# A hybrid decoder trunk: gates and branch products with tokens on partitions, 512 features at a time

## The chip, the cores and the metric

The kernel runs on one core of one Trainium2 chip. The metric is the device time of one launch in microseconds (us). A core has TensorE (PE in the profile; its weight loads have a row of their own, PEld), VectorE (DVE), ScalarE (ACT), GpSimd (POOL) and SyncE (SP, which here issues the loads). SBUF has 128 partitions; TensorE writes to PSUM alone, and its results are read from there by VectorE or ScalarE.

## What is computed

Two layers; in each, three attention mixers, merged by gates, then an output projection, and an MLP. All is float32, with 256 tokens and 1024 features. The part that the change touches, cut from the reference:

```python
h = _rms_norm(x, norm_mix_pre[l])
proj = jnp.einsum('bsd,de->bse', h, w_in[l])
dq, dk, dv, mq, mk, mv, c_q, c_kv, k_pe, g = jnp.split(proj, IN_OFFSETS, axis=-1)
... # oa, ob, oc: the three mixers, each (B, S, 512)
branches = jnp.stack([oa, ob, oc], axis=2)
br = jnp.einsum('bsgc,gcd->bsgd', branches, w_branch[l])   # w_branch: (3, 512, 1024)
gates = jax.nn.sigmoid(g.reshape(B, S, N_BRANCH, D_MODEL)) # 3 x 1024 features
mixed = jnp.einsum('bsd,de->bse', jnp.sum(gates * br, axis=2), w_out[l])
x = x + _rms_norm(mixed, norm_mix_post[l])
```

## The kernel before

**Products in three parts.** Each float32 weight is split into two float32r parts: the high part by a ScalarE copy (L129), the low part by a VectorE subtraction (L130), both 1024 columns wide, once for each load (`chunk`, L132). A product is then three matmuls into one PSUM tile: high by high (L176), high by low (L177), low by high (L178), by `mm3` and `mm_group`. The loads go through 5 raw buffers, and the parts through 6 buffers for high and 6 for low.

**Two layouts of a product.** In `load_f` (L167) a load is 4 blocks of 128 rows by 256 columns, the weights are the operand that stays (128 columns), and the activations move, 256 tokens at a time: the result has features on partitions. In `load_t` (L159) a load is 2 blocks of 128 rows by 512 columns, the activations stay (128 tokens), and 512 columns of weights move: the result has tokens on partitions. Either way a matmul is 128 by 128 stationary, and a layout needs no transposed copy of the activations, which lie with features on partitions.

**The stage.** In `mixer`, L624 to 660, for each of four blocks of 256 features and three branches: a gate product over 8 blocks of rows (PSUM tile `pg`, 48 matmuls of 256 columns), multiplied on VectorE by the tokens' 1/rms, which lies along the free axis (`rb2`, L639), into a gate tile of 512 columns `g`. Then, again for each feature block and branch: the sigmoid of the gate on ScalarE (L646), the branch product over 4 blocks of rows (`pb`, 24 matmuls), its product with the gate on VectorE into `br` (L653), and sums over branches on GpSimd (L657). The sum, which already has features on partitions, is split into the high and low part of `mixed` (ScalarE L659, VectorE L660). The output projection (`out_proj`, tiles `po`, 512 columns, tokens on partitions) takes `mixed` as its stationary operand, two of its eight row blocks in each of four `mixed` tiles.

**What sets the order.** A scheduler at build time places the instructions on each engine by a timeline of its own, and after that each engine keeps its order. It puts gate products between the steps of the attention, as filler for TensorE; the stage after the attention is gate products, then branch products, then the output projection. Three of the last five `w_out` loads put their parts in buffers of the gate pool (6 buffers of 1024 columns, L701).

Of the kernel before, what the change touches and what calls it, by code (L numbers as in the profile page):

```python
# [9 lines left out]
F32 = mybir.dt.float32  # L10
# [3 lines left out]
AF = mybir.ActivationFunctionType  # L14
OP = mybir.AluOpType

D = 1024
# [12 lines left out]
            2.7524476990947733e-06, -2.3874981991411914e-08)  # L30
# First relative distance of each T5 bucket that distances 0..255 can reach.
BUCKET_START = tuple(range(17)) + (21, 27, 35, 46, 59, 77, 99, 128, 166, 216)
# [3 lines left out]
def trunk(ctx: ExitStack, tc: tile.TileContext, x, positions, rel_bias, norm_mix_pre, norm_mix_post,  # L36
# [45 lines left out]

# [1 line left out]
    # Rows of vectors that act on features once those lie on partitions.  # L84
    n_rows = 16 + 16 + 4 + 2 + 2
# [37 lines left out]

# [1 line left out]
    def split(dst_hi, dst_lo, src, quick=False):  # L125
# [6 lines left out]
    def chunk(src, nk, c, name, parts=None, spare=None, quick=False):  # L132
        """One load of weights and its two parts; `spare` is a pool that is idle now."""
        n = nk * c
# [24 lines left out]
    def load_t(w2d, c0, c, name, kts=KT):  # L159
        """Weights that move: kts tiles of [128, c]."""  # L160
        nk = 1024 // c
        r = []
        for k0 in range(0, kts, nk):
            r += chunk(wslice(w2d, k0, nk, c0, c), nk, c, f"{name}_{k0}")
        return r

    def load_f(w2d, c0, name, kts=KT):  # L167
        """Weights that stay: two blocks of 128 columns, kts tiles each."""
        r = []
        for k0 in range(0, kts, 4):  # L170
            r += chunk(wslice(w2d, k0, 4, c0, 256), 4, 256, f"{name}_{k0}")
        return [[(h[:, b * 128:(b + 1) * 128], l[:, b * 128:(b + 1) * 128]) for h, l in r] for b in range(2)]
# [15 lines left out]

# [1 line left out]
    def new_act(name):  # L190
# [40 lines left out]
    def post_norm(xt, ps2, wpost, eps_col):  # L231
        """x += rms_norm(ps2) * wpost"""
        parts = small_tile("pnp", 2)
# [18 lines left out]

# [1 line left out]
    bias = consts.tile([128, 9, 256], F32, name="bias")  # L254
# [22 lines left out]
    def setup_rope():  # L277
# [11 lines left out]
        for t in range(2):  # L289
            for j in range(2):  # L290
                V.tensor_scalar(ang[:, t, j, :], fr, pf[:, t:t + 1], None, op0=OP.mult)
        # Index 0: sine.  Index 1: cosine, the sine a quarter turn on.
        V.tensor_scalar(k[:, :, 0, :], ang[:, :, 0, :], 1.0 / math.pi, MAGIC, op0=OP.mult, op1=OP.add)
# [23 lines left out]
    def setup_lam():  # L317
# [10 lines left out]
        for l in range(DEPTH):  # L328
            li = 0.8 - 0.6 * math.exp(-0.3 * l)
            nc.vector.tensor_scalar(lam[:, l:l + 1], dots[:, 2 * l:2 * l + 1], dots[:, 2 * l + 1:2 * l + 2], li,  # L330
                                    op0=OP.subtract, op1=OP.add)
            # The weights come out of the chip negated: the sign goes here.
            nc.vector.tensor_scalar(subc[:, l:l + 1], cols[:, 38 + l:39 + l], -(1.0 - li), None, op0=OP.mult)

# [1 line left out]
    last_exp = [None]  # L336
# [35 lines left out]
    def av_f(ps, pt, v0, v1):  # L372
        """ps [c, 256 queries] = v^T p^T"""
        nc.tensor.matmul(ps, v0, pt[:, 0:256], start=True, stop=False)
        nc.tensor.matmul(ps[:, 128:256], v1, pt[:, 256:384], start=False, stop=True)

# [1 line left out]
    def load_c(l, k1, n):  # L378
# [5 lines left out]
    def mixer(l, xs, tiles, wc, before):  # L384
# [6 lines left out]

        # latent queries, keys and the shared rope key, token-major
        wc = wc or load_c(l, 0, 4)
# [30 lines left out]

        # 1/rms of every token along the free axis, on all partitions
        prb = tr_tile("prb")
# [24 lines left out]

        # transposed latents
        def latents():
# [20 lines left out]

        # differential attention
        o_a = []
# [44 lines left out]

        # block attention: one block holds the whole sequence, so each query sees its own block
        mv = v_proj(OFF['mv'], "mv")
# [14 lines left out]

        # latent attention
        uq = []  # L540
# [85 lines left out]

        # gates and the products of the three branches, two feature blocks at a time
        branches = [[(o[j // 2][:, 0, j % 2, :], o[j // 2][:, 1, j % 2, :]) for j in range(4)] for o in (o_a, o_b, o_c)]
        gs = {}
        for d in range(4):  # L630
            if d % 2 == 0:
                gt2 = [gpool.tile([128, 2, 512], F32, tag="g", name="g") for _ in range(3)]
            for b in range(3):
                w = load_f(win, OFF['g'] + b * D + d * 256, f"g{l}{b}{d}")
                pg = mm_tile("pg")
                for j in range(2):
                    mm_group(pg[:, j * 256:(j + 1) * 256], w[j], act)
                gt = gt2[b][:, d % 2, :]
                nc.vector.tensor_tensor(gt.rearrange("p (b s) -> p b s", b=2), pg.rearrange("p (b s) -> p b s", b=2),  # L639
                                        rb2, op=OP.mult)  # L640
                gs[b, d] = gt
        mixed = new_act("mixed")
        for d in range(4):
            m = None
            for b in range(3):
                i = nc.scalar.activation(gs[b, d], gs[b, d], AF.Sigmoid)  # L646
                order_after(i, sig_after)
                w = load_f(w_branch[l, b], d * 256, f"br{l}{b}{d}", kts=4)
                pb = acc_tile("pb")
                for j in range(2):  # L650
                    mm_group(pb[:, j * 256:(j + 1) * 256], w[j], branches[b])
                r = prep_tile("br")
                nc.vector.tensor_tensor(r, pb[:], gs[b, d], op=OP.mult)  # L653
                if m is None:
                    m = r
                else:
                    nc.gpsimd.tensor_tensor(m, m, r, op=OP.add)  # L657
            mv_ = m.rearrange("p (b s) -> p b s", b=2)
            nc.scalar.activation(mixed[d][:, 0], mv_, AF.Copy)  # L659
            nc.vector.tensor_tensor(mixed[d][:, 1], mv_, mixed[d][:, 0].bitcast(F32), op=OP.subtract)  # L660

        # output projection
        wpost = load_post(norm_mix_post, l, sig_after)
# [14 lines left out]
    def finish(accs, held, xs, wpost, eps_cols, nxt, wcol, stored=None):  # L678
        """The last rows of a projection, the first half of the tokens ahead, and the norm that follows."""
        for t in range(2):  # L680
# [14 lines left out]
    def out_proj(l, w2d, act, wpost, xs):  # L695
        """x += rms_norm(mixed @ w_out); the next block's input follows each half of the tokens."""
        tiles = new_act("h2")
# [143 lines left out]
```

## Time and profile before

| what | value |
|---|---|
| median of 3 runs | 875.62 us (873.63 to 876.04) |
| the profiled execution: span from its first to its last instruction | 874.3 us |
| TensorE: busy, matmuls | 858.1 us (98%), 5820 |
| weight loads of TensorE | 791.0 us (90%) |
| VectorE, ScalarE, GpSimd busy | 62%, 54%, 12% |
| DMA: read, mean rate | 151.19 MB, 175 GB/s |
| granted clock of TensorE, mean of the span | 0.997 of full |

The profile gives no time of the profiled execution beside its span. A matmul's duration on the page is from its issue to a modelled end, and matmuls overlap: for what one costs in a full queue, the time from one start to the next is read, in the view of instructions in order of time.

### The profile page before, as it was taken

What the parts mean: (1) busy time and instruction counts of PE and PEld (TensorE: products, weight loads), DVE (VectorE), ACT (ScalarE), POOL (GpSimd) and SP (SyncE); (2) the same over time, 40 slices, a digit from 0 to 9 for tenths busy, and PEclk for the clock granted to TensorE, in tenths of its full rate; (3) what the DMA queues carried; (4) which work ended last, traced back from release to release, by engine and by line L of the source; (5) the groups of instructions that cost most, each with busy time, mean ns of one, the idle gap of its engine ahead of it and who ended that gap; (6) DMA issues with size and microseconds to landing.
All of it is one profiled execution on the core that took longest, in us unless ns stands there. A gap on an engine that the chain in (4) does not pass through costs nothing.

```text
span 874.3 us, 14960 instructions
## 1 busy us (share of the span) xinstructions
PE 858.1 (98%) x5820; PEld 791.0 (90%) x5820; DVE 539.6 (62%) x921; ACT 468.9 (54%) x820; POOL 107.1 (12%) x130
## 2 busy tenths in 40 slices
PE   7999999999999999999999999999999999999997
PEld 6988999899988999999899899999998899999995
DVE  6757688457867445446575768954578754554452
ACT  6536675644546444445464757664544664444441
POOL 2211210001311000000100012000033010000010
PEclk9999999999999999999999999999999999999999
DMA  8865544356666656667738553546558466665631
GB/s 275 260 168 180 144 124 134 107 178 184 203 232 195 185 182 189 191 193 212 228 97 248 146 149 97 150 117 189 177 187 270 145 218 191 192 193 182 186 115 49
DMA packets 109798, 154.27 MB, mean 176 GB/s; under 512 B 5103, under 2 KB 89136, under 8 KB 109728
## 3 DMA queue, kind: packets, MB, share of 16 engines
q1 hardware_dynamic: 108448, 149.70, 56.4%
q10 hardware_dynamic: 608, 2.11, 0.7%
q0 software_dynamic: 672, 1.51, 0.6%
q8 instruction: 46, 0.75, 0.4%
q14 instruction: 24, 0.20, 0.1%
HBM read 151.19 MB, written 2.11 MB: 175 GB/s over the span
## 4 chain that ended last, share of the span: by engine, by line
PE 88%; issue 4%; DMA 3%; DVE 2%; ACT 1%; POOL 1%; SPq 0%; POOLq 0%; DVEq 0%; ACTq 0%
PE pu L176 7%; PE pu L178 7%; PE pu L177 7%; PE pd L177 6%; PE pd L178 6%; PE pd L176 6%; PE pg L176 5%; PE pg L177 5%; PE pg L178 5%; PE pb L178 3%; PE pb L177 3%; PE pb L176 3%; PE pmqk L178 2%; PE pmqk L177 2%; PE pmqk L176 2%
## 5 line engine op out<-in xcount | busy, mean ns | idle before, releaser
L177 PE MATMUL pu<-h,hi_up 128*128 128x256 f32 x448 | 126.9, 283 | 0.0
L178 PE MATMUL pu<-h,lo_up 128*128 128x256 f32 x448 | 126.8, 283 | 0.0
L176 PE MATMUL pu<-h,hi_up 128*128 128x256 f32 x448 | 126.7, 283 | 0.0
L130 DVE TENSOR_TENSOR lo_wd<-raw_wd,hi_wd 128x1024 fp32r<-128x1024 f32 x64 | 77.7, 1225 | 74.5 <-ACT hi_wd L129 74.5
L129 ACT ACTIVATE hi_wd<-raw_wd 128x1024 fp32r<-128x1024 f32 x64 | 67.0, 1058 | 82.6 <-PE pu L177 38.0
L176 PE MATMUL pg<-h,hi_g 128*128 128x256 f32 x384 | 110.6, 288 | 0.4 <-ACT lqk L602 0.4
L178 PE MATMUL pg<-h,lo_g 128*128 128x256 f32 x384 | 109.7, 286 | 0.0
L177 PE MATMUL pg<-h,hi_g 128*128 128x256 f32 x384 | 109.1, 284 | 0.0
L130 DVE TENSOR_TENSOR lo_up<-raw_up,hi_up 128x1024 fp32r<-128x1024 f32 x64 | 80.2, 1258 | 38.8 <-ACT hi_up L129 38.5
L129 ACT ACTIVATE hi_up<-raw_up 128x1024 fp32r<-128x1024 f32 x64 | 67.9, 1064 | 59.5 <-PE pu L177 29.0
L176 PE MATMUL pd<-hi_wd,u 128*128 128x512 f32 x256 | 99.9, 390 | 0.0
L177 PE MATMUL pd<-lo_wd,u 128*128 128x512 f32 x256 | 99.8, 390 | 0.0
L178 PE MATMUL pd<-hi_wd,u 128*128 128x512 f32 x256 | 99.6, 389 | 0.0
L176 PEld LDWEIGHTS pu<-h,hi_up 128*128 128x128 f32 x448 | 85.9, 192 | 0.6
L177 PEld LDWEIGHTS pu<-h,hi_up 128*128 128x128 f32 x448 | 85.9, 192 | 0.5
L178 PEld LDWEIGHTS pu<-h,lo_up 128*128 128x128 f32 x448 | 85.9, 192 | 0.1
L130 DVE TENSOR_TENSOR lo_g<-raw_g,hi_g 128x1024 fp32r<-128x1024 f32 x48 | 58.6, 1222 | 39.0 <-ACT hi_g L129 38.7
L176 PEld LDWEIGHTS pg<-h,hi_g 128*128 128x128 f32 x384 | 73.5, 191 | 1.4 <-ACT lqk L602 0.6
L177 PEld LDWEIGHTS pg<-h,hi_g 128*128 128x128 f32 x384 | 73.5, 191 | 0.5 <-issue 0.3
L178 PEld LDWEIGHTS pg<-h,lo_g 128*128 128x128 f32 x384 | 73.5, 191 | 0.1
L129 ACT ACTIVATE hi_g<-raw_g 128x1024 fp32r<-128x1024 f32 x48 | 50.5, 1057 | 40.2 <-PE pg L177 32.2
L752 POOL TENSOR_TENSOR r<-r 128x512 f32<-128x512 f32 x28 | 30.6, 1094 | 262.1 <-ACT u L751 230.9
(293 smaller groups left out, 2109.2 us busy)
## 6 DMA issues: line engine op xcount, KB each, us to landing
raw_up<-in_w_up_dram SPq DMA_DIRECT2D x64, 512.0 KB, 3.9
raw_wd<-in_w_down_dram SPq DMA_DIRECT2D x64, 512.0 KB, 4.2
raw_g<-in_w_in_dram SPq DMA_DIRECT2D x48, 512.0 KB, 3.8
raw_br<-in_w_branch_dram SPq DMA_DIRECT2D x24, 512.0 KB, 4.1
raw_dqk<-in_w_in_dram SPq DMA_DIRECT2D x16, 512.0 KB, 5.2
raw_mqk<-in_w_in_dram SPq DMA_DIRECT2D x16, 512.0 KB, 4.1
raw_wo<-in_w_out_dram SPq DMA_DIRECT2D x16, 512.0 KB, 3.9
raw_dv<-in_w_in_dram SPq DMA_DIRECT2D x8, 512.0 KB, 4.9
```

Source lines behind the costliest of these rows:

```text
L129: nc.scalar.activation(dst_hi, src, AF.Copy)
L130: nc.vector.tensor_tensor(dst_lo, src, dst_hi.bitcast(F32), op=OP.subtract)
L176: i = nc.tensor.matmul(ps, sh, mh, start=first, stop=False)
L177: nc.tensor.matmul(ps, sh, ml, start=False, stop=False)
L178: nc.tensor.matmul(ps, sl, mh, start=False, stop=last)
L752: nc.gpsimd.tensor_tensor(r, r, r, op=OP.mult)
```

## The change

The gates and the branch products go from `load_f` to `load_t`: tokens on partitions, 512 features in one matmul. A gate tile is now two token tiles of 512 features for each half of the features and each branch; its 1/rms is one number for each partition, so a ScalarE copy with a scale (L637) takes over from the VectorE multiplication. The product with the gate is written in place into the gate tile, GpSimd sums in place, and the sum, which has tokens on partitions, is transposed on TensorE (four 128 by 128 transposes for each half and token tile, PSUM tile `pmx`, L657) and split into `mixed` from there (L662, L663). The comments of the file are left out too. The core of the diff:

```diff
-        for d in range(4):
-            if d % 2 == 0:
-                gt2 = [gpool.tile([128, 2, 512], F32, tag="g", name="g") for _ in range(3)]
+        for hf in range(2):
             for b in range(3):
-                w = load_f(win, OFF['g'] + b * D + d * 256, f"g{l}{b}{d}")
-                pg = mm_tile("pg")
-                for j in range(2):
-                    mm_group(pg[:, j * 256:(j + 1) * 256], w[j], act)
-                gt = gt2[b][:, d % 2, :]
-                nc.vector.tensor_tensor(gt.rearrange("p (b s) -> p b s", b=2), pg.rearrange("p (b s) -> p b s", b=2),
-                                        rb2, op=OP.mult)
-                gs[b, d] = gt
+                w = load_t(win, OFF['g'] + b * D + hf * 512, 512, f"g{l}{b}{hf}")
+                gt2 = gpool.tile([128, 2, 512], F32, tag="g", name="g")
+                for t in range(2):
+                    pg = mm_tile("pg")
+                    mm_group(pg[:], toks(act, t), w)
+                    nc.scalar.activation(gt2[:, t, :], pg[:], AF.Copy, scale=rr[:, t:t + 1])
+                    gs[hf, b, t] = gt2[:, t, :]
...
-                w = load_f(w_branch[l, b], d * 256, f"br{l}{b}{d}", kts=4)
-                pb = acc_tile("pb")
-                for j in range(2):
-                    mm_group(pb[:, j * 256:(j + 1) * 256], w[j], branches[b])
-                r = prep_tile("br")
-                nc.vector.tensor_tensor(r, pb[:], gs[b, d], op=OP.mult)
...
-            mv_ = m.rearrange("p (b s) -> p b s", b=2)
-            nc.scalar.activation(mixed[d][:, 0], mv_, AF.Copy)
-            nc.vector.tensor_tensor(mixed[d][:, 1], mv_, mixed[d][:, 0].bitcast(F32), op=OP.subtract)
+                w = load_t(w_branch[l, b], hf * 512, 512, f"br{l}{b}{hf}", kts=4)
+                for t in range(2):
+                    g = gs[hf, b, t]
+                    i = nc.scalar.activation(g, g, AF.Sigmoid)
+                    order_after(i, sig_after)
+                    pb = acc_tile("pb")
+                    mm_group(pb[:], toks(branches[b], t), w)
+                    nc.vector.tensor_tensor(g, pb[:], g, op=OP.mult)
+                    if b:
+                        m = gs[hf, 0, t]
+                        nc.gpsimd.tensor_tensor(m, m, g, op=OP.add)
+            for t in range(2):
+                m = gs[hf, 0, t]
+                pt = tr_tile("pmx")
+                for j in range(4):
+                    nc.tensor.transpose(pt[:, j * 128:(j + 1) * 128], m[:, j * 128:(j + 1) * 128], ident[:])
+                for p in range(2):
+                    hi = mixed[2 * hf + p][:, 0, :, t * 128:(t + 1) * 128]
+                    lo = mixed[2 * hf + p][:, 1, :, t * 128:(t + 1) * 128]
+                    v = pt[:, p * 256:(p + 1) * 256].rearrange("p (b s) -> p b s", b=2)
+                    nc.scalar.activation(hi, v, AF.Copy)
+                    nc.vector.tensor_tensor(lo, v, hi.bitcast(F32), op=OP.subtract)
```

Where it moves instructions. First TensorE, where the last gate product of layer 0 meets the first branch product (`h`: the block's input; `hi_g`, `lo_g`: the parts of gate weights; `oa`: the first mixer's output; `hi_br`, `lo_br`: the parts of branch weights). Before:

```order
L176 MATMUL pg_2373<-h3_148,hi_g023_4_2369 128x256
L177 MATMUL pg_2373<-h3_148,hi_g023_4_2369 128x256
L178 MATMUL pg_2373<-h3_148,lo_g023_4_2370 128x256
L176 MATMUL pb_2434<-oa0_725,hi_br000_0_2430 128x256
L177 MATMUL pb_2434<-oa0_725,hi_br000_0_2430 128x256
L178 MATMUL pb_2434<-oa0_725,lo_br000_0_2431 128x256
```

And now:

```order
L176 MATMUL pg_2109<-hi_g021_6_2078,h3_148 128x512
L177 MATMUL pg_2109<-lo_g021_6_2079,h3_148 128x512
L178 MATMUL pg_2109<-hi_g021_6_2078,h3_148 128x512
L176 MATMUL pb_2152<-hi_br000_0_2141,oa0_725 128x512
L177 MATMUL pb_2152<-lo_br000_0_2142,oa0_725 128x512
L178 MATMUL pb_2152<-hi_br000_0_2141,oa0_725 128x512
```

The two operands have changed places, and each matmul is 512 columns wide: there are 576 `pg` and 288 `pb` matmuls in place of 1152 and 576.

Second TensorE at the start of the output projection of layer 0 (`po`: its four accumulators; `hi_wo`, `lo_wo`: parts of its weights). Before, the 9th to 15th row after the last `pb`:

```order
L178 MATMUL po00_2863<-hi_wo0_1_2887,mixed0_2423 128x512
L176 MATMUL po01_2864<-hi_wo0_1_2887,mixed0_2423 128x512
L177 MATMUL po01_2864<-lo_wo0_1_2888,mixed0_2423 128x512
L176 MATMUL po10_2865<-hi_wo0_0_2869,mixed0_2423 128x512
L177 MATMUL po10_2865<-lo_wo0_0_2870,mixed0_2423 128x512
L178 MATMUL po10_2865<-hi_wo0_0_2869,mixed0_2423 128x512
L178 MATMUL po01_2864<-hi_wo0_1_2887,mixed0_2423 128x512
```

And now, the 20th to 31st row after the last `pb`:

```order
L657 MATMUL pmx_2417<-ident_99,g_1928 128x128 x4
L177 MATMUL po00_2447<-lo_wo0_2_2490,mixed1_2136 128x512
L178 MATMUL po00_2447<-hi_wo0_2_2489,mixed1_2136 128x512
L176 MATMUL po01_2448<-hi_wo0_2_2489,mixed1_2136 128x512
L177 MATMUL po01_2448<-lo_wo0_2_2490,mixed1_2136 128x512
L176 MATMUL po11_2450<-hi_wo0_0_2453,mixed0_2135 128x512
L177 MATMUL po11_2450<-lo_wo0_0_2454,mixed0_2135 128x512
L178 MATMUL po11_2450<-hi_wo0_0_2453,mixed0_2135 128x512
L176 MATMUL po11_2450<-hi_wo0_1_2471,mixed0_2135 128x512
L177 MATMUL po11_2450<-lo_wo0_1_2472,mixed0_2135 128x512
L178 MATMUL po11_2450<-hi_wo0_1_2471,mixed0_2135 128x512
L657 MATMUL pmx_2426<-ident_99,g_1928 128x128 x4
```

The transposes of the second half of the features stand in TensorE's queue among the first matmuls of the projection, 19 and 29 matmuls behind the last `pb`; those of the first half stand among the `pb` matmuls of the second half, each 29 matmuls behind the last one of the branch product that they need.

Third VectorE at the same place, from its last product with a gate on. Before:

```order
L653 TENSOR_TENSOR br_2846<-pb_2821,g_2050 128x512
L130 TENSOR_TENSOR lo_wo0_5_2936<-raw_wo0_5_2933,hi_wo0_5_2935 128x1024
L130 TENSOR_TENSOR lo_up0_0_3098<-raw_up0_0_3095,hi_up0_0_3097 128x1024
L660 TENSOR_TENSOR mixed3_2426<-br_2777,mixed3_2426 128x512
L130 TENSOR_TENSOR lo_up0_2_3104<-raw_up0_2_3101,hi_up0_2_3103 128x1024
```

And now:

```order
L649 TENSOR_TENSOR g_2082<-pb_2402,g_2082 128x512
L130 TENSOR_TENSOR lo_up0_0_2682<-raw_up0_0_2679,hi_up0_0_2681 128x1024
L663 TENSOR_TENSOR mixed2_2137<-pmx_2417,mixed2_2137 128x2x128
L663 TENSOR_TENSOR mixed3_2138<-pmx_2417,mixed3_2138 128x2x128
L130 TENSOR_TENSOR lo_wo0_5_2520<-raw_wo0_5_2517,hi_wo0_5_2519 128x1024
L130 TENSOR_TENSOR lo_up0_2_2688<-raw_up0_2_2685,hi_up0_2_2687 128x1024
L130 TENSOR_TENSOR lo_up0_4_2694<-raw_up0_4_2691,hi_up0_4_2693 128x1024
L663 TENSOR_TENSOR mixed2_2137<-pmx_2426,mixed2_2137 128x2x128
```

The low parts of `mixed` are now four narrow pieces for a half of the features, each behind its transposes, and `lo_wo_5`, which goes into a gate buffer that the last transposes read, stands between them.

## Rows read from the trace of the kernel before

**Rows 1.** The page: busy time, share and count of each engine.

```profile
PE 858.1 (98%) x5820; PEld 791.0 (90%) x5820; DVE 539.6 (62%) x921; ACT 468.9 (54%) x820; POOL 107.1 (12%) x130
```

**Rows 2.** The page: the chain that ended last, share of the span by engine.

```profile
PE 88%; issue 4%; DMA 3%; DVE 2%; ACT 1%; POOL 1%; SPq 0%; POOLq 0%; DVEq 0%; ACTq 0%
```

**Rows 3.** Waits of TensorE: total us, times, longest.

```profile
PE pu L176 <- DVE h L211: 1.2, 2, 0.6
PE ppt L361 <- DVE e L369: 0.5, 1, 0.5
PE pg L176 <- ACT lqk L602: 0.4, 1, 0.4
```

**Rows 4.** Stretches: busy PE, PEld, DVE, ACT, POOL; PEclk, DMA share, GB/s.

```profile
170.00:203.20 33.20, 33.20 (x279) 33.20 (x279) 15.41 (x18) 14.83 (x17) 0.00 (x0) 1.00 0.62 183
203.20:238.00 34.80, 34.80 (x292) 34.80 (x291) 28.00 (x29) 16.71 (x18) 10.54 (x6) 1.00 0.62 189
310.00:340.00 30.00, 30.00 (x179) 26.80 (x178) 14.65 (x15) 14.24 (x16) 3.12 (x3) 1.00 0.63 194
```

**Rows 5.** Groups by line and shape: count, busy us, mean ns, idle before.

```profile
L177 PE MATMUL pg<-h,hi_g 128*128 128x256 f32 x384 | 109.1, 284 | 0.0
L176 PE MATMUL pb<-oa,hi_br 128*128 128x256 f32 x64 | 18.1, 283 | 0.0
```

**Rows 6.** In order of time: first and last of layer 0's 288 `pb`.

```profile
203.29 0.28 PE L176 MATMUL pb<-oa,hi_br 128*128 128x256 f32 x1
...
237.73 0.28 PE L178 MATMUL pb<-oc,lo_br 128*128 128x256 f32 x1
```

**Rows 7.** In order of time: 24 `pd` from first to last; 8 `pdv`.

```profile
287.69 0.39 PE L176 MATMUL pd<-hi_wd,u 128*128 128x512 f32 x1
...
292.91 0.39 PE L178 MATMUL pd<-hi_wd,u 128*128 128x512 f32 x1
...
460.22 0.39 PE L177 MATMUL pdv<-lo_dv,h 128*128 128x512 f32 x1
...
461.81 0.39 PE L178 MATMUL pdv<-hi_dv,h 128*128 128x512 f32 x1
```

**Rows 8.** In order of time: a group of four transposes between `pu` matmuls.

```profile
279.43 0.28 PE L176 MATMUL pu<-h,hi_up 128*128 128x256 f32 x1
279.55 0.60 PE L733 MATMUL put<-ident,r 128*128 128x128 f32 x4
279.91 0.36 PE L177 MATMUL pu<-h,hi_up 128*128 128x256 f32 x1
280.11 0.28 PE L178 MATMUL pu<-h,lo_up 128*128 128x256 f32 x1
```

**Rows 9.** Groups by line and shape on ScalarE, VectorE and GpSimd.

```profile
L129 ACT ACTIVATE hi_br<-raw_br 128x1024 fp32r<-128x1024 f32 x24 | 25.4, 1060 | 28.7 <-PE pg L177 15.1 <-PE pb L177 12.3 <-ACT hi_br L129 1.4
L130 DVE TENSOR_TENSOR lo_br<-raw_br,hi_br 128x1024 fp32r<-128x1024 f32 x24 | 33.3, 1387 | 18.9 <-ACT hi_br L129 18.7
L438 ACT ACTIVATE mv<-pmv,rr 128x512 f32<-128x512 f32 x4 | 2.7, 682 | 1.0 <-PE pmv L178 1.0
L639 DVE TENSOR_TENSOR g<-pg,rb 128x512 f32<-128x512 f32 x24 | 16.4, 684 | 0.6 <-PE pg L178 0.5
L653 DVE TENSOR_TENSOR br<-pb,g 128x512 f32<-128x512 f32 x24 | 16.4, 684 | 4.8 <-PE pb L178 4.8
L738 ACT ACTIVATE u<-put 128x256 fp32r<-128x256 f32 x8 | 3.0, 377 | 0.7 <-DVE u L739 0.7
L739 DVE TENSOR_TENSOR u<-put,u 128x256 fp32r<-128x256 f32 x8 | 3.4, 419 | 0.9 <-ACT u L738 0.9
```

**Rows 10.** In order of time: the end of layer 0's branch stage, all engines.

```profile
239.54 0.69 DVE L653 TENSOR_TENSOR br<-pb,g 128x512 f32<-128x512 f32 x1
...
238.64 4.37 POOL L657 TENSOR_TENSOR br<-br 128x512 f32<-128x512 f32 x2 [4.40 <-DVE br L653]
...
243.04 0.63 ACT L659 ACTIVATE mixed<-br 128x512 fp32r<-128x512 f32 x1 [2.50 <-POOL br L657]
```

More of the change, by code (lines that the diff above doesn't have):

```diff
@@ L642, in mixer @@
         mixed = new_act("mixed")
-        for d in range(4):
-            m = None
+        for hf in range(2):
             for b in range(3):
-                i = nc.scalar.activation(gs[b, d], gs[b, d], AF.Sigmoid)
-                order_after(i, sig_after)
-                w = load_f(w_branch[l, b], d * 256, f"br{l}{b}{d}", kts=4)
-                pb = acc_tile("pb")
-                for j in range(2):
-                    mm_group(pb[:, j * 256:(j + 1) * 256], w[j], branches[b])
-                r = prep_tile("br")
-                nc.vector.tensor_tensor(r, pb[:], gs[b, d], op=OP.mult)
[L654 to L657, printed above, removed]
-            mv_ = m.rearrange("p (b s) -> p b s", b=2)
-            nc.scalar.activation(mixed[d][:, 0], mv_, AF.Copy)
-            nc.vector.tensor_tensor(mixed[d][:, 1], mv_, mixed[d][:, 0].bitcast(F32), op=OP.subtract)
+                w = load_t(w_branch[l, b], hf * 512, 512, f"br{l}{b}{hf}", kts=4)
[20 more added lines that the diff above has]
+                    nc.vector.tensor_tensor(lo, v, hi.bitcast(F32), op=OP.subtract)
```

## The prediction, made before the changed kernel was run

> **What bounds the kernel now.** I read the busy times first: TensorE is busy for 858.1 of 874.3 us [rows 1], and the chain that ended last lies on it for 88% [rows 2]. Busy time alone proves little, since matmuls overlap in it, so the waits of TensorE came next: the one in the gate products is 0.4 us in all, and the longest that any of the three rows names is 0.6 us [rows 3]. Then the stage that is changed, by stretches: from the end of layer 0's attention to its output projection TensorE is busy for every microsecond, at a granted clock of 1.00, which is the 2.4 GHz level, while VectorE and ScalarE have room: 15.4 and 14.8 of 33.2 us in the gate products, 28.0 and 16.7 of 34.8 in the branch products [rows 4]. So here time is what TensorE's queue takes, matmul by matmul, and a microsecond less of it is a microsecond of the span as long as nothing comes late in its place.
>
> What a matmul takes is its step, from one start to the next. Layer 0's 288 branch matmuls start between 203.29 and 237.73 us, 287 steps in 34.44: **120.0 ns at 256 columns** [rows 6]. For 512 columns, 24 matmuls of the down projection take 23 steps in 5.22 us, and eight `pdv`, which already have the tokens stationary and the weights moving as the change wants it, 7 steps in 1.59: **227.0 and 227.1 ns** [rows 7]. Twice 120.0 is 240.0. So merging two matmuls of 256 columns into one of 512 takes off 13 ns: a fixed part of each instruction that twice the columns do not double.
>
> **The change part by part.**
>
> *Matmuls.* There are 1152 gate matmuls (three lines of 384) and 576 branch matmuls (nine groups of 64) of 256 columns [rows 5]; 864 of 512 take their place. 864 x (240.0 - 227.0) ns = **11.2 us less**, all of it on TensorE's queue. The bounds: 227 is the nearest row, `pdv` being the same form; if in this place a wide matmul took as much as two narrow ones, nothing would come off. I take 227.
>
> The Trainium skill (TensorE: Matmul & The Clock Gate, Back-to-back issue gap) speaks against the change: it gives the isolated gap at full clock as the columns over 2.4 GHz plus 2.5 ns, so a merged pair would give back 2.5 ns, an estimate of 2.2 us in all. By that rule the rows would read 109 and 216 ns; they read 120.0 and 227.0, so the fixed part here is some 13 ns, and the rows decide.
>
> *Transposes.* New on TensorE: two halves of the features, two token tiles, two layers, so 8 groups of four. Such a group stands in the MLP: from 279.43 to 280.11 us there are two `pu` matmuls and one group; 0.68 less 2 x 0.12 is **0.44 us a group**, the slower step after it included [rows 8]. Eight make **3.5 us more**. TensorE has no idle time to hide them in. If each also had to wait, the nearest price is the longest wait of `pu` for a transposed input, 0.6 us [rows 3]: 4.8 us on top. I take no wait, for the reason under the second rival.
>
> *Evacuations.* 24 VectorE multiplications of gates, 684 ns each, go (16.4 us), and 24 ScalarE copies with a scale come, of the kind of `mv`, 682 ns [rows 9]. The products with the gate and the sums on GpSimd stay as many. Where the sum is split, 8 wide pieces on each engine become 16 narrow ones at 377 ns on ScalarE and 419 ns on VectorE [rows 9]: 6.0 and 6.7 us over both layers. VectorE, the busier of the two, is relieved. All of this lies beside TensorE and counts nothing as long as it does; uncovered, a pair of pieces would cost 0.8 us.
>
> *Loads.* As many and as large as before. A load feeds 12 matmuls of 227 ns, 2.72 us, where it fed 24 of 120, 2.88 us: 193 GB/s in place of 182. The MLP, where the down projection already eats a load in 12 such matmuls, moves 194 GB/s without a gap on TensorE [rows 4]. No cost.
>
> *Order.* TensorE's order differs in the gate and branch stages alone. Between the steps of the attention there are now fewer and longer runs of gate products. There are 24 such runs where there were 32. The step after a change of kind reads 0.20 us in place of 0.12 [rows 8]; eight of those are 0.6 us less, which I leave to the range.
>
> **Sum.** 11.2 less and 3.5 more: 7.7 us off. Against the profiled execution: 874.3 - 7.7 = 866.6. Its span lies 1.3 us below the median of the runs; against that, 875.6 - 7.7 = **867.9 us**, 0.9% faster. What is late next is TensorE again.
>
> **The rivals.**
>
> *First: weights come late (slower).* A half of the features needs all of a branch's 8 row blocks, four loads, for the first token tile and again for the second. So four of the six buffers for parts are tied up where it was two. The third load of the next group can be split only when the first of this one has been used for the second token tile, 6 matmuls into it. From there to the third load's first use there are 18 matmuls of this group and 12 of the next, 30 x 0.227 = 6.8 us; the split takes 1.06 on ScalarE and 1.39 on VectorE [rows 9], so 4.3 us are left for what stands ahead in the two queues. ScalarE now has the gate copies there as well, and a burst of sigmoids after the last exponential. There are 12 gate groups in two layers: the gain is eaten from 7.7 / 12 = 0.64 us of wait per group on. If each waited for one subtraction more, 1.39 us, 16.7 us would be lost, and the time would be 884.6. Against it: both engines are less than half busy in the gate products [rows 4], and their queues there hold little more than these splits. I give it 6%.
>
> *Second: the transposes wait at the head of TensorE's queue.* A group of transposes needs the last product with the gate on VectorE and the sum on GpSimd. In the trace that product at 239.54 us takes 0.69, two sums take 4.37, and the copy follows at 243.04 [rows 10]: one sum may take 2.2 us, so 0.7 + 2.2 and up to 1.4 for a subtraction ahead in VectorE's queue, 4.3 us. Each group stands at least 29 matmuls behind its last branch product, 29 x 0.227 = 6.6 us. So 2.3 us of slack. Behind the transposes the first `mixed` piece of the second half is needed some 20 matmuls later, 4.5 us against 0.8 for a pair of pieces and one subtraction of 1.4. If it went wrong by 0.6 us for each of 8 groups, 4.8 us: 872.7, still a little faster. 5%.
>
> *Third: the wide matmul is no cheaper than the two that it replaces.* This is the mechanism of the first bound, and the page's rule above comes close to it: the fixed part would be small, and the 13 ns an accident of other stages. Then only the transposes are left: 875.6 + 3.5 = 879.1, slower; it decides from a step of 236 ns on. Against it stand `pdv` and `pd` at 227 in two stages, with DMA as busy as here. 4%.
>
> *Fourth: more comes off,* since the longer runs between the steps of the attention leave TensorE fewer waits and switches. At most all of it: 32 switches at 0.08 us and the waits of 0.5 and 0.4 us there [rows 3, 8], 3.5 us: 864.4. 5%.
>
> **How the numbers follow.** The forecast has 80%, and its own spread is what the runs differ by (1.2 us either way) and a microsecond or two for switches: 865 to 871. With the second rival's 872.7 and the upper part of the fourth, the range is **864.5 to 872.8**. It leaves out the first and third rival and a little of the fourth. A measurement of this kernel can tell 0.3%, 2.6 us, from no change. Faster by more: the forecast, the fourth and most of the second, 0.88. Within it: the rest of the second, and mild forms of the first and third, 0.06. Slower by more: 0.06.
>
> **What would show it.** In the profile after: steps of 227 ns in `pg` and `pb`, with 288 `pb` matmuls over two layers; 32 transposes into `pmx` in groups of 0.44 us with no idle time before them; the stretch from the first to the last `pb` shorter by 1.9 us in each layer before the transposes count; VectorE's busy time down by some 15 us and ScalarE's up by 17. The prediction is wrong if a step is 236 ns or more, if TensorE's waits name `hi_g`, `lo_g` or `lo_br` (first rival) or the sum in `g` (second), or if the stages before and after the change move by more than a microsecond.

## The result, and the profile after

The changed kernel takes **864.17 us** (median of four runs, 863.19 to 865.59) against 875.12 for the kernel before in the same runs: a ratio of 0.988 (95% interval, here and below in brackets: [0.9865, 0.9897]), 10.95 us or 1.2% off. It is faster, as forecast, but by 3.7 us more than the 867.9 that I named, and the median lies 0.3 us below the lower end of the range (864.5); the interval, 863.3 to 866.1 us on 875.12, does not tell it from that end. Later the changed kernel was timed once more beside the kernel before: 865.06 against 875.58 (the median of five runs; a sixth, in a slow state at a granted clock of 0.56, took 1410.98 us and is left out), a ratio of 0.989 [0.9867, 0.9906].

The page of the changed kernel, busy time of each engine and the chain that ended last; they answer to [rows 1, 2]:

```profile
PE 846.5 (98%) x4988; PEld 744.2 (86%) x4988; DVE 522.6 (61%) x905; ACT 482.3 (56%) x852; POOL 107.4 (12%) x130
PE 88%; issue 4%; DMA 3%; DVE 2%; ACT 1%; POOL 1%; SPq 0%; POOLq 0%; DVEq 0%; ACTq 0%
```

The span is 861.3 us. TensorE still bounds the kernel with the same shares; it issues 832 matmuls fewer (864 merged away, 32 transposes new). VectorE is 17.0 us less busy, ScalarE 13.4 more.

Three of the six rows of TensorE's waits in the changed kernel, in total us, times, longest; they answer to [rows 3]:

```profile
PE pu L176 <- DVE h L211: 1.2, 2, 0.6
PE ppt L361 <- DVE e L369: 0.5, 1, 0.5
PE pg L176 <- ACT lqk L602: 0.4, 1, 0.4
```

The same three rows with the same numbers. The other three, which the kernel before has too, are waits for the first loads (`pcols`, `pin`) and for a softmax (`ppt`, L495). No row of the six names `hi_g`, `lo_g`, `lo_br` or `g`: nothing waits for weights, and no transpose waits for a sum.

The groups of the changed stages, by line and shape (count, busy us, mean ns, idle before); they answer to [rows 5, 9]:

```profile
L176 PE MATMUL pg<-hi_g,h 128*128 128x512 f32 x192 | 76.0, 396 | 0.4 <-ACT lqk L602 0.4
L176 PE MATMUL pb<-hi_br,oa 128*128 128x512 f32 x32 | 12.5, 389 | 0.0
L657 PE MATMUL pmx<-ident,g 128*128 128x128 f32 x32 | 4.8, 272 | 0.0
L637 ACT ACTIVATE g<-pg,rr 128x512 f32<-128x512 f32 x24 | 16.5, 686 | 25.6 <-PE pg L178 25.6
L662 ACT ACTIVATE mixed<-pmx 128x256 fp32r<-128x256 f32 x16 | 5.7, 372 | 2.8 <-DVE mixed L663 2.8
L663 DVE TENSOR_TENSOR mixed<-pmx,mixed 128x256 fp32r<-128x256 f32 x16 | 6.5, 419 | 6.0 <-ACT mixed L662 6.0
```

The 32 transposes of line 657 have 0.0 us of idle time before them, and the new pieces on ScalarE and VectorE take what their models in [rows 9] take.

In order of time, four branch matmuls that follow each other, then a group of transposes between branch matmuls (start, us, line, names):

```profile
200.20 0.39 PE L176 MATMUL pb<-hi_br,ob 128*128 128x512 f32 x1
200.42 0.39 PE L177 MATMUL pb<-lo_br,ob 128*128 128x512 f32 x1
200.65 0.39 PE L178 MATMUL pb<-hi_br,ob 128*128 128x512 f32 x1
200.88 0.39 PE L176 MATMUL pb<-hi_br,ob 128*128 128x512 f32 x1
...
214.02 0.39 PE L177 MATMUL pb<-lo_br,oa 128*128 128x512 f32 x1
214.26 0.60 PE L657 MATMUL pmx<-ident,g 128*128 128x128 f32 x4
214.61 0.48 PE L178 MATMUL pb<-hi_br,oa 128*128 128x512 f32 x1
214.92 0.40 PE L176 MATMUL pb<-hi_br,oa 128*128 128x512 f32 x1
```

Three steps in 0.68 us: 227 ns. From 214.02 to 214.92 there are two matmuls and one group: 0.90 less 2 x 0.227 is 0.45 us for the group.

The whole branch stage of layer 0, from its first branch matmul to the first of the projection (busy PE, PEld, DVE, ACT, POOL; PEclk, DMA share, GB/s), the changed kernel:

```profile
194.08:227.68 33.60, 33.60 (x154) 27.80 (x152) 24.06 (x29) 16.70 (x20) 10.39 (x6) 1.00 0.71 219
```

and the kernel before, the same piece, which begins and ends with [rows 6]:

```profile
203.29:237.85 34.56, 34.56 (x290) 34.56 (x289) 27.76 (x29) 16.71 (x18) 10.54 (x6) 1.00 0.62 189
```

33.60 us, two groups of transposes included, in place of 34.56; without the two groups 32.70, which is 1.9 us less. TensorE is busy for all of it at the same granted clock, 1.00.

**Where the time went.** I added up TensorE's steps, each from one matmul's start to the next one's and put down to the first of the two, from the last `pmqk` (an input product of the second mixer) to the first `pu` (the MLP), over both layers. "Attention" is everything there that has no column of its own: what is left of the second mixer, and the latent attention with its value products.

| us, both layers | attention | `pg` | `pb` | `pmx` | `po` | `pin` | sum |
|---|---|---|---|---|---|---|---|
| before | 54.33 | 142.54 | 69.12 | | 43.78 | 1.58 | 311.35 |
| after | 51.25 | 134.96 | 65.78 | 2.84 | 44.37 | 2.09 | 301.29 |
| after - before | -3.08 | -7.58 | -3.34 | +2.84 | +0.59 | +0.51 | -10.06 |

The four columns from `pg` to `po` are the sum of the forecast: -7.49 measured, -7.7 forecast. Two columns were not in it: **attention, which the change does not touch, is 3.1 us shorter**, and `pin`, the transposes of the next norm, are 0.5 longer. In all 10.06 us of the 10.95; the rest, 0.9 us, lies outside these stages and is within the interval of the ratio (9.0 to 11.8 us; the ratio itself, 0.9881, is 10.4).

Where the 3.1 us are, the groups of the value products of the latent attention show, in the kernel before:

```profile
L374 PE MATMUL sc<-pt,vl 128*64 128x256 f32 x32 | 7.8, 404 | 0.0
L375 PE MATMUL sc<-pt,vl 128*64 128x128 f32 x32 | 4.6, 272 | 0.0
```

and in the changed one:

```profile
L374 PE MATMUL sc<-pt,vl 128*64 128x256 f32 x32 | 5.3, 405 | 0.0
L375 PE MATMUL sc<-pt,vl 128*64 128x128 f32 x32 | 3.2, 273 | 0.0
```

As many instructions, each as long, and yet 3.9 us less busy time: more of them run at the same time. Each head has one matmul in each of the two lines, two records each in the trace, with 64 output columns; the two heads of a pair write partitions 0 to 63 and 64 to 127 of one PSUM tile. In order of time, two heads apart, in the kernel before:

```profile
150.75 0.65 PE L374 MATMUL sc<-pt,vl 128*64 128x256 f32 x2
151.23 0.38 PE L375 MATMUL sc<-pt,vl 128*64 128x128 f32 x2
151.55 0.55 PE L361 MATMUL ppt<-ident,e 128*128 128x128 f32 x3
```

two heads that already stand side by side there:

```profile
159.87 0.66 PE L374 MATMUL sc<-pt,vl 128*64 128x256 f32 x4
160.36 0.39 PE L375 MATMUL sc<-pt,vl 128*64 128x128 f32 x4
```

and two heads side by side in the changed kernel:

```profile
160.13 0.66 PE L374 MATMUL sc<-pt,vl 128*64 128x256 f32 x4
160.62 0.40 PE L375 MATMUL sc<-pt,vl 128*64 128x128 f32 x4
160.94 0.87 PE L361 MATMUL ppt<-ident,e 128*128 128x128 f32 x6
```

Two heads, four records of either line (x4), take 0.81 us from the first start to that of the transposes behind; one head, half as many records (x2), takes 0.80. Whether the heads of a pair stand side by side is the scheduler's doing: in the order of the kernel before 4 of the 8 pairs do, in the new order all 8. The scheduler had other gate products to put between the steps of the attention; that these made the difference is tested first below.

### The profile page after: what moved, and what is told of

Same layout as the page of the kernel before. It is cut to its first block, busy times and chain, and to the rows that moved or that the text cites. A ratio compares the mean times of both kernels' runs of the same rounds, so it can differ in the third digit from the quotient of the medians.

```text
span 861.3 us, 13257 instructions
## 1 busy us (share of the span) xinstructions
PE 846.5 (98%) x4988; PEld 744.2 (86%) x4988; DVE 522.6 (61%) x905; ACT 482.3 (56%) x852; POOL 107.4 (12%) x130
## 4 chain that ended last, share of the span: by engine, by line
PE 88%; issue 4%; DMA 3%; DVE 2%; ACT 1%; POOL 1%; SPq 0%; POOLq 0%; DVEq 0%; ACTq 0%
PE pu L176 7%; PE pu L178 7%; PE pu L177 7%; PE pd L176 7%; PE pd L177 6%; PE pd L178 6%; PE pg L176 5%; PE pg L177 5%; PE pg L178 5%; PE pb L177 3%; PE pb L178 3%; PE pb L176 3%; PE pmqk L178 2%; PE po L178 2%; PE pmqk L177 2%
## 5 line engine op out<-in xcount | busy, mean ns | idle before, releaser
L130 DVE TENSOR_TENSOR lo_up<-raw_up,hi_up 128x1024 fp32r<-128x1024 f32 x64 | 78.1, 1223 | 38.8 <-ACT hi_up L129 38.8
L176 PE MATMUL pg<-hi_g,h 128*128 128x512 f32 x192 | 76.0, 396 | 0.4 <-ACT lqk L602 0.4
L178 PE MATMUL pg<-hi_g,h 128*128 128x512 f32 x192 | 76.2, 397 | 0.0
L177 PE MATMUL pg<-lo_g,h 128*128 128x512 f32 x192 | 75.5, 393 | 0.0
L178 PEld LDWEIGHTS pd<-hi_wd,u 128*128 128x128 f32 x256 | 48.1, 188 | 10.2
L652 POOL TENSOR_TENSOR g<-g 128x512 f32<-128x512 f32 x16 | 29.4, 1850 | 219.0 <-DVE g L649 219.0
L176 PEld LDWEIGHTS pd<-hi_wd,u 128*128 128x128 f32 x256 | 48.1, 188 | 9.6
L177 PEld LDWEIGHTS pd<-lo_wd,u 128*128 128x128 f32 x256 | 48.1, 188 | 9.4
```

The costliest lines, as they stand in the source:

```text
L130: nc.vector.tensor_tensor(dst_lo, src, dst_hi.bitcast(F32), op=OP.subtract)
L176: i = nc.tensor.matmul(ps, sh, mh, start=first, stop=False)
L177: nc.tensor.matmul(ps, sh, ml, start=False, stop=False)
L178: nc.tensor.matmul(ps, sl, mh, start=False, stop=last)
L652: nc.gpsimd.tensor_tensor(m, m, g, op=OP.add)
```

## The experiments

The theory after the first look: two causes, the merged matmuls less their transposes (7.5 us), and the pairs that now run side by side (3.1). The rival: the pairs are beside the point, and the matmuls gave more than the forecast, or the attention lost waits. All runs are timed beside the kernel before; "the steps" are sums as in the table above.

### Gates alone, branch alone

The first takes the new gates (`load_t`, tokens on partitions) and keeps the old branch products:

```diff
-        for d in range(4):
+        for hf in range(2):
             for b in range(3):
-                w = load_f(win, OFF['g'] + b * D + d * 256, f"g{l}{b}{d}")
-                pg = mm_tile("pg")
-                for j in range(2):
-                    mm_group(pg[:, j * 256:(j + 1) * 256], w[j], act)
...
+                w = load_t(win, OFF['g'] + b * D + hf * 512, 512, f"g{l}{b}{hf}")
+                gt2 = gpool.tile([128, 2, 512], F32, tag="g", name="g")
+                for t in range(2):
+                    pg = mm_tile("pg")
+                    mm_group(pg[:], toks(act, t), w)
+                    nc.scalar.activation(gt2[:, t, :], pg[:], AF.Copy, scale=rr[:, t:t + 1])
+                    gs[b, 2 * hf + t] = gt2[:, t, :]
```

> The gate products alone go to tokens on partitions and 512 columns; the branch products stay as before. Gates and branch products then meet in tiles of different layouts, so this kernel multiplies numbers that do not belong together; each instruction has its size. No transposes. First theory (matmul steps and the order of the attention): 576 merged pairs x 13 ns = 7.5 us off; TensorE's order in the attention stage is that of the changed kernel, with all eight pairs of the latent attention's value products (L374, L375, two heads in one PSUM tile) side by side where the kernel before has four, worth 0.6 us each, and some 0.8 us of switches: together 10.6 us off, 864.5. Rival (the gain beyond the 7.7 us of the prediction lies in parts that the change does not touch): 7.5 us off, 867.6.

863.59 against 875.11, ratio 0.987 [0.9851, 0.9897]: as much as the whole change. By the steps `pg` is 7.57 us shorter and attention 3.07, and the first line of its value products is that of the changed kernel:

```profile
L374 PE MATMUL sc<-pt,vl 128*64 128x256 f32 x32 | 5.3, 405 | 0.0
```

The second keeps the old gates and takes the new branch products with their transposes:

> The branch products alone go to tokens on partitions, with the transposes of their sum; the gate products stay as before, with features on partitions, so products and gates of different layouts meet, as in the run of the gates alone; each instruction has its size. TensorE's order in the attention stage is that of the kernel before. First theory: 288 merged pairs x 13 ns = 3.7 us off, 8 groups of transposes x 0.44 = 3.5 us on: 0.2 us off, 875. Rival (the gain of the change beyond the forecast is in the branch stage): 3 us off, 872.

874.86 against 875.11, ratio 1.000 [0.9984, 1.0011]: nothing. By the steps `pb` gives 3.28 us, `pmx` and `po` take 3.44, `pin` takes 0.50, and attention stays at 54.33 (four of eight pairs side by side). So the branch half of the change pays for its own transposes and no more, and what the attention gains comes with the gates, which are what stands between its steps.

### Without the transposes

```diff
-                pt = tr_tile("pmx")
-                for j in range(4):
-                    nc.tensor.transpose(pt[:, j * 128:(j + 1) * 128], m[:, j * 128:(j + 1) * 128], ident[:])
...
-                    v = pt[:, p * 256:(p + 1) * 256].rearrange("p (b s) -> p b s", b=2)
+                    v = m[:, p * 256:(p + 1) * 256].rearrange("p (b s) -> p b s", b=2)
```

> The changed kernel without its 32 transposes: the sum with tokens on partitions goes as it is into the pieces of the projection's input, so the projection gets its input untransposed; its work is left in full. First theory: 8 groups at 0.44 us come off the changed kernel's 864.2, 3.5 us: 860.7, 14.4 us under the kernel before. Rival (the transposes hide, or pay by their wait as well): 864 or under 859.

860.14, ratio 0.983 [0.9815, 0.9852]: 4.0 us below the changed kernel. By the steps `pmx` is gone (2.84), `pb` is 0.50 and `po` 0.65 shorter, which are the slower steps behind a group (with the transposes, the first step behind a group is 313 to 318 ns in place of 227, and most of the next seven are 228 to 236), and `pin` is back at 1.58. So by the steps eight groups cost 4.0 us, 0.50 each; with `pin` and the rest the stages are 4.4 shorter, which the runs' 4.0 does not tell apart. The merged matmuls alone give 7.5 in `pg` and 69.12 - 65.28 = 3.8 in `pb`, 11.4 in all, or 13.2 ns for each of 864.

### The value products, in pairs and apart

In the kernel before, both heads' transposes first, and then the value products of the pair in one go; `av_f` puts its first matmul behind the instruction in `after` and returns its last:

```diff
-                for par, (h, _, e) in enumerate(hs):
-                    pt = transpose_p(e)
-                    vs = slice(h * 64, (h + 1) * 64)
-                    av_f(po[par * 64:(par + 1) * 64, :256], pt, vl[:, 0, vs], vl[:, 1, vs])
+                pts = [transpose_p(e) for _, _, e in hs]
+                done = None
+                for par in (1, 0):
+                    vs = slice(hs[par][0] * 64, (hs[par][0] + 1) * 64)
+                    done = av_f(po[par * 64:(par + 1) * 64, :256], pts[par], vl[:, 0, vs], vl[:, 1, vs], after=done)
```

> The kernel before, with one thing of the order changed: in the latent attention both heads of a pair are transposed first, and their value products stand side by side on TensorE, all eight pairs over the two layers where four of eight do so in the kernel before. First theory (two value products that fill different halves of one tile's partitions run at the same time when they stand side by side): four pairs x 0.6 us, 2.4 us off: 872.7. Rival (order in the attention is worth nothing, TensorE is full anyway): 875.1.

871.02 against 875.11, ratio 0.996 [0.9944, 0.997]: 4.1 us, without any of the change. Its groups (the lines have moved: 378 and 381 are 374 and 375):

```profile
L378 PE MATMUL sc<-pt,vl 128*64 128x256 f32 x32 | 5.3, 405 | 0.0
L381 PE MATMUL sc<-pt,vl 128*64 128x128 f32 x32 | 3.2, 272 | 0.0
```

These are the busy times of the changed kernel. By the steps the stages are 3.7 us shorter: 3.1 in the value products, as four pairs give below, and 0.6 in other steps that the new order moved. Next the reverse in both kernels: each head's transposes come behind the value product of the head before.

```diff
+                done = None
                 for par, (h, _, e) in enumerate(hs):
-                    pt = transpose_p(e)
+                    pt = transpose_p(e, after=done)
...
-                    av_f(po[par * 64:(par + 1) * 64, :256], pt, vl[:, 0, vs], vl[:, 1, vs])
+                    done = av_f(po[par * 64:(par + 1) * 64, :256], pt, vl[:, 0, vs], vl[:, 1, vs])
```

The kernel before, so edited:

> The same rule in the kernel before: none of the eight pairs of value products stands side by side, where four do. First theory: 4 x 0.6 = 2.4 us on 875.1: 877.5. So that, between this kernel and the changed one without pairs, only matmul widths and transposes differ: 8 us apart. Rival: 875.1.

878.91 against 875.67, ratio 1.005 [1.0028, 1.0065]: 3.2 us slower (4.1 by the steps, 3.1 of it in the value products). Now no two heads are side by side:

```profile
L378 PE MATMUL sc<-pt,vl 128*64 128x256 f32 x32 | 10.3, 405 | 0.0
L381 PE MATMUL sc<-pt,vl 128*64 128x128 f32 x32 | 6.1, 273 | 0.0
```

The changed kernel, so edited:

> The changed kernel, with one thing of the order changed: in the latent attention the second head of a pair is transposed only after the value products of the first, so that no two value products of a pair stand side by side, where all eight pairs do in the changed kernel. First theory (side by side they overlap, 0.6 us a pair): 8 x 0.6 = 4.8 us on the changed kernel's 864.2: 869.0. Rival: no difference, 864.2.

867.68, ratio 0.992 [0.99, 0.9938]: 3.5 us slower than the changed kernel (4.0 by the steps, 3.1 of it in the value products). The edit did only half of what it was meant to: the heads of one pair are apart, but four times the second head of a pair came to stand beside the first head of the next one, and there they overlap as well. Such a place, in order of time:

```profile
160.05 0.66 PE L378 MATMUL sc<-pt,vl 128*64 128x256 f32 x4
160.53 0.40 PE L381 MATMUL sc<-pt,vl 128*64 128x128 f32 x4
160.86 0.87 PE L361 MATMUL ppt<-ident,e 128*128 128x128 f32 x6
```

Again 0.81 us for two heads, which here write two PSUM tiles. So the overlap does not hang on the shared tile. Whether it needs different halves of the partitions no run tells: in every such place one head writes the lower half and the other the upper. The steps of the value products in the three cases: none side by side 12.71 us, four times 9.59, eight times 6.47 (the changed kernel, and the kernel before in pairs). That is a straight line, 3.12 us for four: a pair takes 1.59 us apart and 0.81 side by side, **0.78 us saved a pair**. The expectations had put it at 0.6, from the first look at a few places.

### Which property of the wide matmul

In the changed kernel, with the pairs held together, every wide gate and branch matmul is cut into two of 256 columns, with the same tokens stationary and the weights moving:

```diff
-                    mm_group(pg[:], toks(act, t), w)
+                    for c in (0, 256):
+                        mm_group(pg[:, c:c + 256], toks(act, t), [(wh[:, c:c + 256], wl[:, c:c + 256]) for wh, wl in w])
...
-                    mm_group(pb[:], toks(branches[b], t), w)
+                    for c in (0, 256):
+                        mm_group(pb[:, c:c + 256], toks(branches[b], t), [(wh[:, c:c + 256], wl[:, c:c + 256]) for wh, wl in w])
```

> The changed kernel, tokens on partitions as they are and transposes too, but each gate and branch matmul of 512 columns made as two of 256 with the same stationary operand; all eight pairs of value products are held side by side. First theory (an instruction has a fixed part of 13 ns, whatever stays and whatever moves): 864 more matmuls x 13 ns = 11.2 us on the changed kernel's 864.2, and some tenths for more switches in the attention (42 runs of gate products for 24): 875.4 to 876.5, as slow as the kernel before; steps of 120 ns in both products. Rival (it is the operand that stays that makes the step, not the width): steps near 114 ns and 864 to 866.

874.03 against 874.45, ratio 1.000 [0.9984, 1.0008]. Rows from its branch stage:

```profile
205.53 0.28 PE L176 MATMUL pb<-hi_br,oa 128*128 128x256 f32 x1
...
207.69 0.28 PE L176 MATMUL pb<-hi_br,ob 128*128 128x256 f32 x1
```

18 steps in 2.16 us: 120 ns, as in the kernel before. By the steps `pg` and `pb` are 212.5 us, which is 11.8 more than in the changed kernel and 0.9 more than in the kernel before. The run is slower by only some 10 of these, and 1.4 us below what was expected: in this order attention is another 1.1 us shorter, and `pin` is back at 1.59. What pays is the number of matmuls, not which operand stays. In each of these kernels every matmul has a weight load of its own (5820 of either before, 4988 after, 5852 here), so no run tells whether the fixed part belongs to the matmul or to its load.

### The half microsecond in `pin`

The norm behind the projection writes `x` in two halves, and `pin` transposes them. The changed kernel, all engines, in order of time:

```profile
246.16 1.41 DVE L250 SCALAR_TENSOR_TENSOR x<-yw,pnq,x 128x512 f32<-128x512 f32 x2
...
247.02 0.42 PEld L201 LDWEIGHTS pin<-ident,x 128*128 128x128 f32 x4 [0.28 <-issue]
247.06 1.29 PE L201 MATMUL pin<-ident,x 128*128 128x128 f32 x8
...
247.69 0.42 PEld L201 LDWEIGHTS pin<-ident,x 128*128 128x128 f32 x4 [0.24 <-PE pin L201]
```

VectorE ends the second half of `x` at 246.16 + 1.41 = 247.57, and the second four loads of `pin` begin at 247.69, 0.24 us after the first four were done. The row names `pin` itself as what ended that time, and the list of waits has no line for this wait; by its times it is the second half of `x`, for which TensorE has come to `pin` too early. To test that I tried the changed kernel with two of the held-back weight blocks of the projection in gate buffers instead of three, which changes the order of the projection's matmuls:

```diff
-            spare = (gpool, "g") if KT - HELD <= k < KT - HELD + 3 else None
+            spare = (gpool, "g") if KT - HELD <= k < KT - HELD + 2 else None
```

> The changed kernel with the sixth of the eight output weight loads (k = 5) in the common buffers for parts, and no longer in gate buffers that the last transposes read. The first token half of the projection can then end earlier, and the norm's input has 15 matmuls of cover in place of 12. If the 0.25 us that the transposes of x wait for the norm in each layer is due to this: 0.5 us off the changed kernel, 863.7. If the weight load now waits for a common buffer: equal or up to 2 us more.

863.86, ratio 0.988 [0.9855, 0.9897]. The trace shows what was meant:

```profile
246.29 1.42 DVE L250 SCALAR_TENSOR_TENSOR x<-yw,pnq,x 128x512 f32<-128x512 f32 x2
...
247.60 1.02 PEld L201 LDWEIGHTS pin<-ident,x 128*128 128x128 f32 x8
247.83 1.04 PE L201 MATMUL pin<-ident,x 128*128 128x128 f32 x8
```

`pin` takes 1.04 us in place of 1.29, with its eight loads in one row, and 1.58 over both layers by the steps. 0.5 us is too little for the runs to tell: 863.86 and 864.17 are the same time to them.

### Both together

The changed kernel with the pairs held by the edit above and two blocks in gate buffers:

> The changed kernel with both orders put together: all pairs of value products held side by side, transposed first, and the sixth output weight load in the common buffers. The pairs stand side by side in the changed kernel as well, so the first theory gives the 0.5 us of the transposes' wait, and nothing for the pairs: 863.7; up to 1 us more if the longer groups of transposes save switches.

863.78 against 875.58, ratio 0.987 [0.985, 0.9888]. The scheduler had already paired all heads in the changed kernel, so holding them gives no time. That it would keep a later change from losing it is not shown.

## Why the prediction was right, and where its size was off

**Bound and sign: right.** TensorE's queue was the bound before and is the bound after; a step taken off it came off the time.

**Merged matmuls: right.** Forecast 11.2 us from 864 x 13 ns; measured 11.4 (the changed kernel without transposes). The step is 227 ns in the changed stages at a granted clock of 1.00, and cutting the matmuls again gives 120 ns and, in these two products, takes all of it back. The third rival (a wide matmul no cheaper) is out. The rule of the Trainium skill (TensorE: Matmul & The Clock Gate, Back-to-back issue gap) that the prediction weighed would have made it 2.2 us, an estimate; the measured 11.4 decides against it.

**Transposes: a little low.** Forecast 3.5 us at 0.44 a group, measured 4.0 at 0.50. The row of [rows 8] from which I took 0.44 counts one slower step behind the group; by the run without transposes, and by the steps behind a group, more than one step there is a little longer. None waited, so the second rival is out: the order that the prediction read (29 matmuls behind the last branch product) was cover enough.

**Evacuations and loads: right.** They are beside TensorE: no wait names them. VectorE fell by 17.0 us (forecast some 15) and ScalarE rose by 13.4 (forecast 17). The forecast had added up the durations of instructions, and by that sum ScalarE rose by 17.2 (516.9 to 534.1 us); the page's busy time counts overlapping instructions once. The first rival, weights that come late, did not happen: `hi_g`, `lo_g` and `lo_br` appear in no wait.

**Order: this is the step that failed.** The prediction says that TensorE's order differs in the gate and branch stages alone; it differs in the attention too. It counted the runs of gate products between the steps of the attention, 24 in place of 32, at 0.08 us a change of kind, 0.6 us, and left that to the range. What the new order moved was something else, the attention's own matmuls: all eight pairs of value products now stand side by side instead of four, at 0.78 us a pair, 3.1 us. Of the 3.08 us that the attention lost, 3.12 are in these steps, so the fewer changes of kind gave nothing that can be seen. The fourth rival had the place and nearly the size (up to 3.5 us, 864.4, 5%), but by another mechanism: that the result came out near its 864.4 is luck. The chance of more coming off was far too low. The profile of the kernel before already held it: the same two lines as x2 in one place and as x4, in the same time, in another (150.75 and 159.87 us, above). I read the order of the changed kernel only for the engines' hand-overs in the gate and branch stages, and not for the lines that the change leaves alone. One of the signs of being wrong that I had named, stages before and after the change that move by more than a microsecond, came true.

On what the overlap is, the trace says that the matmuls of two heads, 64 output columns each in either half of the partitions, take the time of one head's. The Trainium skill (TensorEngine Tiling (Array Packing), Key Properties) says that different tiles of the array work independently and can run matmuls in parallel. The trace agrees, if the two heads' 64 columns are two such tiles: 0.81 us for both heads against 0.80 for one.

**Not forecast: `pin`.** The new order of the projection leaves less work between the end of the first token tile's sums and `pin`, 12 matmuls against 15 in the order that has no wait; 0.5 us.

**The sum.** 7.7 forecast. To it come 3.1 (pairs) and 0.2 (matmuls), and from it go 0.5 (transposes) and 0.5 (`pin`): 10.0, where the steps give 10.06. The other 1.4 us between forecast and result are 0.5 by which the median of the kernel before fell (875.62 to 875.12) and 0.9 outside the stages. The span of the kernel before, 874.3 us, fits only the slowest of its runs, 876.04 us: in every other run on record a span lies at least 1.7 us below its time. So it lay 1.7 us below its own time, not 1.3 as the prediction took it against the median. The profiled spans differ by 13.0 us, 2.9 of them outside the stages, and these lie ahead of them, in layer 0's first part: the MLPs and the other stages between and behind agree within 0.1 us. There the kernel before has this stretch (busy PE, PEld, DVE, ACT, POOL; PEclk, DMA share, GB/s):

```profile
70.00:80.00 10.00, 8.02 (x56) 7.82 (x55) 9.86 (x26) 9.37 (x24) 0.87 (x4) 0.83 0.49 133
```

and the changed one:

```profile
70.00:80.00 10.00, 8.64 (x74) 8.44 (x74) 9.66 (x17) 9.10 (x25) 1.73 (x4) 1.00 0.57 173
```

TensorE was idle there for 2.0 us in the one and 1.4 in the other, and the granted clock in that stretch was 0.83 (between the 1.2 and the 2.4 GHz level) against 1.00. The other profiles say that this dip does not hang on the change. The changed kernel with cut matmuls has it, and the kernel before with its heads in pairs does not:

```profile
70.00:80.00 10.00, 7.55 (x52) 7.35 (x51) 9.56 (x29) 8.78 (x23) 0.87 (x4) 0.83 0.40 106
70.00:80.00 10.00, 8.35 (x72) 8.15 (x71) 9.86 (x21) 9.17 (x25) 2.66 (x4) 1.00 0.54 157
```

From the first matmul to the last `pmqk` of layer 0 the two profiles with the dip take 100.3 and 101.3 us, and the nine others 96.5 to 99.3, with the gates of before (97.7 to 99.3) and with the new ones (96.5 to 98.6). So this part varies between profiles of one kind by more than the 0.9 us; what those are stays open.

## What to carry to other kernels

When a scheduler sets the order, compare the new order with the old one also for the instructions that the diff does not touch: here they gave 3.1 of 10 us, and a small edit that holds the pairs together gives the kernel before 4.1 us by itself. On a queue that never idles, count instructions: the same products in half as many matmuls save the fixed part of each one, and a step that must be bought with transposes (here the branch half, 3.8 us for 4.0) may be worth nothing alone. Look for groups whose busy time differs between two kernels at the same count and the same mean, and ask which neighbours made it so.

## What was not expected of the hardware

- Two heads' value products that write different halves of the partitions overlapped wherever they stood next to each other in TensorE's queue, heads of different pairs and PSUM tiles too: 0.81 us for two heads, 1.59 apart.
- At a granted clock of 1.00 the step of these matmuls is 120.0 ns at 256 columns and 227.0 at 512, so that 256 more columns cost 107.0 ns and 13.0 ns of a step do not go with the width. The 120 ns are the same with weights or with tokens stationary.
- A group of four transposes costs 0.50 us, not only its own steps (0.355, 2.84 us in eight groups): the matmuls behind it come later too.
